# A time-mixing kernel: transposed input for batches 10 to 15 from the DMA crossbar, out of a staging copy in DRAM

## The chip, the cores and the metric

The kernel runs on one core of a Trainium2 chip. A core has five instruction streams that matter here: TensorE (PE: matmuls and, against an identity matrix, transposes), VectorE (DVE), ScalarE (ACT), GpSimd (POOL) and SyncE (SP, which only issues transfers). Sixteen DMA engines move data; SP's transfers go out on one queue, POOL's on another; in this kernel POOL's loads convert fp32 to bf16 on the way. The metric is device time in microseconds, the median of several runs.

## The reference

The input `x` has 16 batches of 2048 tokens with 256 features, in fp32. Cut to what matters:

```python
x_prev[:, 1:, :] = x[:, :-1, :]                 # the token before, zero for the first
xv = x * time_mix_v + x_prev * (1 - time_mix_v)
xr = x * time_mix_r + x_prev * (1 - time_mix_r)
v = xv @ value_weight
r = xr @ receptance_weight
out = (sigmoid(r) * v) @ output_weight
```

The key branch (`xk`, `k`) feeds nothing that is returned.

## The kernel before, in words

**Units.** A unit is 512 tokens, a quarter of a batch; there are 64, and the main loop runs over them with index `g`. Matmuls contract over the features, so `x` is needed with features on the partitions: each unit is transposed into a tile `xt`, in bf16. A batch of `xt` has a slot for each 128 tokens and one slot ahead of them, which holds the last 128 tokens moved on by one (the shift); with it, "the token before" is the same tile read one slot earlier.

**Per unit.** The weights carry the mix factors, so what is left to form is `mix = xt(previous) * c + xt`, for `r` and for `v`. One half of the products is scaled on DVE (line 271) or, late in the kernel, on ACT (line 530), the other half on POOL (line 281, `scale_pool`); DVE adds (line 293). Then PE projects (line 301), ACT takes the sigmoid (line 550), DVE multiplies (line 603), PE multiplies by the output weight (line 325), ACT copies the result to SBUF (line 359) and SP stores a pair of units (line 335).

**Two ways to transpose.** For units 1 to 43 PE transposes six units ahead of use (`advance`, `transposes`, line 215), and ACT copies from PSUM (line 232). For the last five batches (`BYDMA`, 20 units) the crossbar of the DMA engines transposes whole batches from the bf16 input tile in SBUF to `xt`: `by_dma`, line 196, issued by SP at units 38, 39, 43, 47 and 51. The first of them, batch 11, is split in two and waits for the last load of all. From unit 38 (`CROSS`) on, ACT does the shift of a batch (line 569) and some of the scales.

**Order.** The order of each engine's instructions is written by hand: an engine takes them in program order and waits at each for what it needs. So an instruction that waits on SP holds up the stores behind it, and one that waits on POOL holds up the scales behind it. `load(b)` is issued by POOL (lines 107 to 120); input tiles have six buffers, so batch `b+5` is loaded when batch `b` begins to be transposed. `WAITING` holds back some stores to set their order against the transposes; `kept` holds them till then. The pools: `xpool` 6 batches of input, `xtpool` 3 batches of `xt`, `opool` 3 batches of output.

Of the kernel before, what the change touches and what calls it, by code (L numbers as in the profile page):

```python
# [8 lines left out]
FP32 = mybir.dt.float32  # L9
BF16 = mybir.dt.bfloat16  # L10
# [5 lines left out]
def kernel(  # L16
# [25 lines left out]
    nc = tc.nc  # L42

    B, S, D = x.shape
    P = 128
    KO = D // P
# [6 lines left out]
    BYUNIT = 2  # L53
    LONG = 8
    H = UJ // 2
    BYDMA = 5 * UB
    CROSS = NU - BYDMA - LOOK
    FREE = CROSS
    LATE_O = CROSS - 2
    WAITING = {33: 38, 35: 39, 37: 43, 39: 43, 45: 51, 47: 51}  # L60
    START_T = [1, 3, 5, 6, 7, 9, 11, 12]
    AHEAD = 6
    PAIRS = 10
    WARM = 25
    WARM2 = 7
    SHIFT_ACT = (8,)

    consts = ctx.enter_context(tc.tile_pool(name="consts", bufs=1))
    xpool = ctx.enter_context(tc.tile_pool(name="xpool", bufs=6))
    xtpool = ctx.enter_context(tc.tile_pool(name="xtpool", bufs=3))  # L70
    mixpool = ctx.enter_context(tc.tile_pool(name="mixpool", bufs=3))
    zpool = ctx.enter_context(tc.tile_pool(name="zpool", bufs=3))
    opool = ctx.enter_context(tc.tile_pool(name="opool", bufs=3))
    ps_t_pool = ctx.enter_context(tc.tile_pool(name="ps_t", bufs=2, space=bass.MemoryType.PSUM))
    ps_v_pool = ctx.enter_context(tc.tile_pool(name="ps_v", bufs=1, space=bass.MemoryType.PSUM))
    ps_r_pool = ctx.enter_context(tc.tile_pool(name="ps_r", bufs=1, space=bass.MemoryType.PSUM))
# [6 lines left out]
    shifted = []  # L83
    kept = {}
    x_bf = {}
    xt = {}
    mix = {}
    o_sb = {}
# [9 lines left out]
    def rows(b):  # L98
        return x[b].rearrange("(p j) d -> p j d", p=P)

    def unit_rows(t, b, e, n=1):

        return t[b, e * TU : (e + n) * TU, :].rearrange("(e p j) d -> p e j d", p=P, j=UJ)

    def load(b):
        if b not in x_bf:
            x_bf[b] = xpool.tile([P, J, D], BF16, name="x_bf")
        if b < BYUNIT:
            for e in range(UB):
                nc.gpsimd.dma_start(  # L110
                    out=x_bf[b][:, e * UJ : (e + 1) * UJ, :], in_=unit_rows(x, b, e)[:, 0]
                )
            return
        if b < B - 1:
            run = 8192 if b < LONG else 16384
            return nc.gpsimd.dma_start(out=x_bf[b], in_=rows(b), max_dma_last_dim=run)  # L116
        return [
            nc.gpsimd.dma_start(out=x_bf[b][:, j : j + J // 2], in_=rows(b)[:, j : j + J // 2])
            for j in (0, J // 2)
        ]  # L120

    x_unit = opool.tile([P, 2, UJ, D], FP32, name="o_sb")
    tm_rows = consts.tile([2 * KO, P], FP32)
# [21 lines left out]
    w_bf = consts.tile([P, 2, KO, D], BF16)  # L145
    w_prev = consts.tile([P, KO, D], BF16)
    wo_bf = consts.tile([P, KO, D], BF16)
    x_first = consts.tile([P, 2, UJ, D], BF16)
    for e in (2, 3):
        op = nc.gpsimd.dma_start(out=x_first[:, e - 2], in_=unit_rows(x, 0, e)[:, 0])  # L150
        if e == 2:
# [11 lines left out]
    warm_up(WARM)  # L163

    def new_xt(b):
        if b < BYUNIT:
            xt[b] = consts.tile([P, UB * (UJ + 1), KO, P], BF16, name=f"xt_first{b}")
        else:
            xt[b] = xtpool.tile([P, J + 1, KO, P], BF16, name="xt")
        (nc.vector if b == 0 else nc.gpsimd).memset(xt[b][:, 0, :, 0:1], 0.0)  # L170

    new_xt(0)
# [18 lines left out]
        nc.vector.reciprocal(c_sb, tms)  # L191
        nc.vector.tensor_scalar(out=c_sb, in0=c_sb, scalar1=-1.0, scalar2=None, op0=ALU.add)

    def by_dma(b, lo, hi, after=None):

        op = nc.sync.dma_start_transpose(
            out=xt[b][:, 1 + lo : 1 + hi].rearrange("p j k c -> p (j k) c"),
            in_=x_bf[b][:, lo:hi].rearrange("p j d -> p (j d)"),
        )
        if after is not None:  # L200
            tc.add_manual_dep(op.ins, after.ins.name, SYNC, reason="not beside a load")

    def transposes(i):

# [125 lines left out]
                stop=(ko == KO - 1),  # L330
            )

    def store(queue, b, lo, hi, after=None):
        dst = out[b].rearrange("(p j) d -> p j d", p=P)
        op = queue.dma_start(out=dst[:, lo:hi, :], in_=o_sb[b][:, lo:hi, :])
        if after is not None:
            tc.add_manual_dep(op.ins, after.ins.name, SYNC, reason="in turn with the last load")

    def out_part(pool, name, z, b, e, jj, n, copy, queue):
        ps = pool.tile([P, n, D], FP32, name=name)  # L340
        for k in range(n):
            out_matmuls(ps, z, jj + k, k)
        lo = e * UJ + jj
        copy(out=o_sb[b][:, lo : lo + n, :], in_=ps)
        store(queue, b, lo, lo + n)

    def output(g, z):
        b, e = divmod(g, UB)
        if e == 0:
            o_sb[b] = opool.tile([P, J, D], FP32, name="o_sb")  # L350
        j0 = e * UJ
        if g >= NU - 4:
            for h in range(2):
                out_part(ps_t_pool, "ps_t", z, b, e, h * H, H, nc.scalar.copy, nc.sync)
            return
        ps = ps_o_pool.tile([P, UJ, D], FP32, name="psum_o")
        for jj in range(UJ):
            out_matmuls(ps, z, jj, jj)
        nc.scalar.copy(out=o_sb[b][:, j0 : j0 + UJ, :], in_=ps)  # L359
        if b < BYUNIT:  # L360
            if e % 2 == 1:
                nc.sync.dma_start(
                    out=unit_rows(out, b, e - 1, 2),
                    in_=o_sb[b][:, j0 - UJ : j0 + UJ, :].rearrange("p (e j) d -> p e j d", j=UJ),
                )
        elif g >= NU - 8:
            store(nc.sync, b, j0, j0 + UJ)
        elif e % 2 == 1:
            pair = (b, j0 - UJ, j0 + UJ)
            if g in WAITING:  # L370
                kept.setdefault(WAITING[g], []).append(pair)
            else:
                store(nc.sync, *pair)

    def last_unit(g):


        b, e = divmod(g, UB)
        s_sb = zpool.tile([P, KO, TU], BF16, name="s_sb")
        z_sb = zpool.tile([P, KO, TU], BF16, name="z_sb")  # L380
        cols = [(h * H * P, (h + 1) * H * P) for h in range(2)]
        spare = [(ps_r_pool, "psum_r"), (ps_t_pool, "ps_t"), (ps_v_pool, "psum_v"), (ps_t_pool, "ps_t")]
        banks = [pool.tile([P, KO, H * P], FP32, name=name) for pool, name in spare]

        by_act, by_dve = nc.scalar.copy, nc.vector.tensor_copy

        def receptance(h):
            lo, hi = cols[h]
            project(banks[h], g, 0, lo, hi)
            nc.scalar.activation(out=s_sb[:, :, lo:hi], in_=banks[h], func=ACT.Sigmoid)  # L390

        def value(h, n):
            lo, hi = cols[h]
            project(banks[2 + h], g, 1, lo, hi)
            for c in range(lo, hi, n * P):
                nc.vector.tensor_tensor(
                    out=z_sb[:, :, c : c + n * P],
                    in0=s_sb[:, :, c : c + n * P],
                    in1=banks[2 + h][:, :, c - lo : c - lo + n * P],
                    op=ALU.mult,  # L400
                )

        receptance(0)
        out_part(ps_o_pool, "psum_o", z_prev, b, e - 1, 0, H, by_dve, nc.sync)
        receptance(1)
        value(0, H)
        out_part(ps_r_pool, "psum_r", z_prev, b, e - 1, H, H, by_act, nc.sync)
        value(1, 1)
        out_part(ps_v_pool, "psum_v", z_sb, b, e, 0, 1, by_act, nc.sync)
        out_part(ps_o_pool, "psum_o", z_sb, b, e, 1, 1, by_act, nc.sync)  # L410
        out_part(ps_t_pool, "ps_t", z_sb, b, e, 2, 1, by_act, nc.scalar)
        out_part(ps_t_pool, "ps_t", z_sb, b, e, 3, 1, by_dve, nc.sync)
# [34 lines left out]
            tc.add_manual_dep(op.ins, after.ins.name, SYNC, reason="one at a time")  # L447

    tnext = 1
    half_load = last_load = None  # L450

    def advance(limit):
        nonlocal tnext, half_load, last_load
        while tnext <= min(limit, NU - 1):
            b, e = divmod(tnext, UB)
            if b == 1 and e > 0:
                load(b + e + 1)
            elif b > 1 and e == 0 and b + 5 < B:
                if b == 2:
                    load(6)  # L460
                last_load = load(b + 5)
                if b + 5 == B - 1:
                    half_load, last_load = last_load
            if tnext < NU - BYDMA:
                transposes(tnext)
            tnext += 1
# [71 lines left out]
    for g in range(NU - 1):  # L538
# [10 lines left out]
        s_sb = zpool.tile([P, KO, TU], BF16, name="s_sb")  # L549
        nc.scalar.activation(out=s_sb, in_=ps_r, func=ACT.Sigmoid)  # L550
        advance(START_T[g] if g < len(START_T) else g + LOOK)
        for b in range(B - 5, B):
            if g == max(UB * (b - 2) - 1, CROSS + (b > B - 5)):
                new_xt(b)
                if b == B - 5:
                    for pair in kept.pop(g):
                        store(nc.sync, *pair, after=half_load)
                    by_dma(b, J - UJ, J, last_load)
                    by_dma(b, 0, J - UJ, last_load)
                else:  # L560
                    by_dma(b, 0, J)
                for pair in kept.pop(g, []):
                    store(nc.sync, *pair)
        by_crossbar = g // UB + 1 if g > CROSS and g % UB == 1 and g < NU - UB else None

        def shift(ko):
# [83 lines left out]
```

## Time and profile before

| | |
|---|---|
| median of 3 runs | 201.58 us (201.2 to 202.09) |
| span of the profiled execution | 199.3 us; a time of the whole call is not listed for that execution |
| PE busy | 194.5 us, 98% |
| DVE busy | 186.1 us, 93% |
| ACT busy | 180.6 us, 91% |
| POOL busy | 83.7 us, 42% |
| SP's DMA queue (q1) | 40.24 MB, 59.0% of 16 engines' span |
| POOL's DMA queue (q0) | 16.39 MB, 41.1% |

The span runs from the first to the last instruction. Busy times are unions over an engine's instructions, so a share near 100% says that the engine hardly stood idle, not that each instruction was at its best. A DMA queue's share is the time that its packets took; the two together come to the whole span. Times to landing are from issue to the last byte's arrival and contain the wait in the queue: the median load of 1024 KB took 24.2 us, the median pair's store 14.4, the median transpose 7.6.

### The profile page before, as it was taken

The numbers are of one execution on the slowest core, as the hardware profiler recorded it, in microseconds if no ns is written. First come the engines' busy times: TensorE is split into PE (matmuls) and PEld (weight loads), VectorE is DVE, ScalarE is ACT, GpSimd is POOL, SyncE is SP. The second block draws the span as 40 slices with busy tenths as digits, with TensorE's granted clock in tenths as the row PEclk, the third lists the DMA queues.
The fourth block names the chain that finished last, engine by engine and source line by source line (L and its number), as shares of the span: only waits on it lengthen the run. The fifth ranks groups of instructions, "written<-read, shape, count | busy, mean of one in ns | idle before, by whom it ended". The sixth has DMA issues, their size and how long they took to land.

```text
span 199.3 us, 3892 instructions
## 1 busy us (share of the span) xinstructions
PE 194.5 (98%) x1421; PEld 125.8 (63%) x1421; DVE 186.1 (93%) x292; ACT 180.6 (91%) x209; POOL 83.7 (42%) x114
## 2 busy tenths in 40 slices
PE   8999999999999999999999999999999999999993
PEld 7765676666666666666666666555666566655671
DVE  0999999999999999899999999999999999999982
ACT  3699899999999999999999999999999999999982
POOL 1846572443443534425434354343444444444200
PEclk9999999999999999999999999999999999999998
DMA  5999999999999999999999999999999999999685
GB/s 182 228 194 217 218 277 275 278 280 274 292 313 293 283 283 288 280 284 284 281 286 337 299 409 294 300 199 226 287 294 396 301 210 261 419 418 409 266 313 213
DMA packets 32442, 57.00 MB, mean 286 GB/s; under 512 B 21796, under 2 KB 23080, under 8 KB 28456
## 3 DMA queue, kind: packets, MB, share of 16 engines
q1 hardware_dynamic: 28208, 40.24, 59.0%
q0 software_dynamic: 4064, 16.39, 41.1%
q8 instruction: 11, 0.18, 0.4%
q10 hardware_dynamic: 152, 0.13, 0.2%
q14 instruction: 7, 0.06, 0.1%
HBM read 34.34 MB, written 33.55 MB: 341 GB/s over the span
## 4 chain that ended last, share of the span: by engine, by line
PE 85%; DVE 10%; issue 1%; POOL 1%; ACT 1%; DVEq 0%; POOLq 0%
PE psum_v L301 25%; PE psum_o L325 24%; PE psum_r L301 24%; PE ps_t L215 7%; DVE z_sb L603 4%; DVE mix L293 3%; DVE mix L271 3%; PE ps_t L161 2%; PE ps_t L325 1%; PE psum_r L243 1%; ACT xt_first L225 1%; PE psum_r L315 0%; PE ps_t L301 0%; POOL x_bf L116 0%; POOL mix L281 0%
## 5 line engine op out<-in xcount | busy, mean ns | idle before, releaser
L281 POOL TENSOR_SCALAR mix<-xt,c_sb 128x1024 bf16<-128x1024 bf16 (+1 forms) x55 | 61.0, 1109 | 91.7 <-DVE mix L293 86.2
L293 DVE TENSOR_TENSOR mix<-mix,xt 128x1024 bf16<-128x1024 bf16 x112 | 77.8, 703 | 1.6
L603 DVE TENSOR_TENSOR z_sb<-s_sb,psum_v 128x1024 bf16<-128x1024 bf16 (+1 forms) x64 | 76.6, 1199 | 2.3 <-PE psum_v L301 0.9
L301 PEld LDWEIGHTS <-w_bf 128*128 128x128 bf16 x516 | 48.7, 98 | 38.9 <-DVE mix L293 1.1
L550 ACT ACTIVATE s_sb<-psum_r 128x1024 bf16<-128x1024 f32 x63 | 65.1, 1033 | 3.6 <-PE psum_r L301 3.3
L359 ACT COPY o_sb<-psum_o 128x1024 f32<-128x1024 f32 x60 | 61.2, 1021 | 6.0 <-PE psum_o L325 6.0
L301 PE MATMUL psum_v<-mix,w_bf 128*128 128x512 bf16 (+1 forms) x256 | 65.3, 377 | 0.5 <-DVE mix L293 0.2
L301 PE MATMUL psum_r<-mix,w_bf 128*128 128x512 bf16 (+1 forms) x252 | 64.2, 377 | 0.1
L325 PE MATMUL psum_o<-wo_bf,z_sb 128*128 128x256 bf16 x486 | 63.2, 272 | 0.0
L325 PEld LDWEIGHTS <-z_sb 128*128 128x128 bf16 x512 | 49.8, 98 | 19.7 <-issue 0.9
L232 ACT COPY xt<-ps_t 128x1024 bf16<-128x1024 bf16 x36 | 36.8, 1033 | 0.0
L215 PEld LDWEIGHTS <-x_bf 128*128 128x128 bf16 x320 | 21.0, 98 | 8.5
L215 PE MATMUL ps_t<-ident,x_bf 128*128 128x128 bf16 x320 | 23.9, 219 | 0.0
L271 DVE TENSOR_SCALAR mix<-xt,c_sb 128x1024 bf16<-128x1024 bf16 (+1 forms) x49 | 22.0, 458 | 0.0
L530 ACT ACTIVATE mix<-xt,c_sb 128x1024 bf16<-128x1024 bf16 x12 | 13.9, 1159 | 0.0
L293 DVE TENSOR_TENSOR mix<-mix,xt_first 128x1024 bf16<-128x1024 bf16 x15 | 10.8, 722 | 0.1
L116 POOL DMA_DIRECT2D x_bf<-in_x_dram x13 | 8.6, 659 | 0.0
L271 DVE TENSOR_SCALAR mix<-xt_first,c_sb 128x512 bf16<-128x512 bf16 x22 | 6.9, 364 | 0.4 <-ACT xt_first L225 0.3
L232 ACT COPY xt_first<-ps_t 128x1024 bf16<-128x1024 bf16 x6 | 6.2, 1028 | 0.0
L281 POOL TENSOR_SCALAR mix<-xt_first,c_sb 128x512 bf16<-128x512 bf16 x6 | 4.1, 684 | 1.6 <-DVE mix L293 1.0
L161 PE MATMUL ps_t<-const-bfloat16-1.0 128*128 128x128 bf16 x32 | 3.8, 312 | 0.8 <-PEq L634 0.8
L443 POOL COPY xt_first<-xt_first 128x254 bf16<-128x254 bf16 x5 | 2.0, 393 | 5.4 <-DVE mix L293 5.3
(70 smaller groups left out, 52.6 us busy)
## 6 DMA issues: line engine op xcount, KB each, us to landing
out_dram<-o_sb SPq DMA_DIRECT2D x28, 1024.0 KB, 14.4
x_bf<-in_x_dram POOLq DMA_DIRECT2D x13, 1024.0 KB, 24.2
out_dram<-o_sb SPq DMA_DIRECT2D x4, 512.0 KB, 2.9
out_dram<-o_sb SPq DMA_DIRECT2D x6, 256.0 KB, 2.5
o_sb<-in_x_dram SPq DMA_DIRECT2D x4, 256.0 KB, 3.6
x_bf<-in_x_dram POOLq DMA_DIRECT2D x4, 256.0 KB, 7.0
x_bf<-in_x_dram POOLq DMA_DIRECT2D x2, 512.0 KB, 10.7
x_first<-in_x_dram POOLq DMA_DIRECT2D x2, 256.0 KB, 4.3
```

Source lines behind the costliest of these rows:

```text
L116: return nc.gpsimd.dma_start(out=x_bf[b], in_=rows(b), max_dma_last_dim=run)
L215: nc.tensor.transpose(out=ps[:, jj], in_=src[:, jj, ko * P : (ko + 1) * P], identity=idn)
L232: nc.scalar.copy(out=xt[b][:, j0 : j0 + UJ], in_=ps)
L271: nc.vector.tensor_scalar(out=mixed(piece)[:, :, ko], in0=xt[b][:, slots(piece), ko], scalar1=c_sb[:, m, ko : ko + 1], scalar2=None, op0=A ...
L281: op = nc.gpsimd.tensor_scalar(out=mixed(piece)[:, :, 1], in0=xt[b][:, slots(piece), 1], scalar1=c_sb[:, m, 1:2], scalar2=1.0, op0=ALU.mul ...
L293: return nc.vector.tensor_tensor(out=mixed(piece), in0=mixed(piece), in1=xt[b][:, slots(piece, 1)], op=ALU.add)
L301: nc.tensor.matmul(out=ps[:, mo, :], lhsT=w_bf[:, m, ko, mo * P : (mo + 1) * P], rhs=mixed((b, m, e * TU + lo, e * TU + hi))[:, :, ko], st ...
L325: nc.tensor.matmul(out=ps[:, slot, :], lhsT=z[:, ko, jj * P : (jj + 1) * P], rhs=wo_bf[:, ko, :], start=(ko == 0), stop=(ko == KO - 1),)
L359: nc.scalar.copy(out=o_sb[b][:, j0 : j0 + UJ, :], in_=ps)
L530: nc.scalar.activation(out=mixed(piece)[:, :, ko], in_=xt[b][:, slots(piece), ko], func=ACT.Copy, scale=c_sb[:, m, ko : ko + 1],)
L550: nc.scalar.activation(out=s_sb, in_=ps_r, func=ACT.Sigmoid)
L603: nc.vector.tensor_tensor(out=z_sb[:, :, c : c + n], in0=s_sb[:, :, c : c + n], in1=ps_v[:, :, c : c + n], op=ALU.mult,)
```

## The change

Six batches instead of five, 10 to 15, go by the crossbar (24 units, so `CROSS` becomes 34). They are no longer loaded into SBUF: POOL's converting load writes them to a tile in DRAM, `x_both`, one for two batches. One transposing transfer takes the 256 rows of such a pair and writes a tile `xt_both` that interleaves the two batches in each slot (128 elements of one, 128 of the other). PE's transposes for the other batches from 2 on write tiles of that form too.

The pair transposes are issued by SP at units 31, 39 and 47 (`T_AT`); each waits for the load issued last. Batches 14 and 15 are loaded at units 35 and 43 (`STAGE_AT`); these loads, on POOL, wait for the transpose issued last. The other loads follow a table (`LOADS`). Output tiles hold two units instead of a batch (nine of them) and are allocated with that size; `xpool` has 4 buffers, one of which first serves as `x_first`; `xtpool` has 2 of double width.

```diff
-    BYDMA = 5 * UB
+    STAGED = 10
+    BYDMA = NU - STAGED * UB
-    WAITING = {33: 38, 35: 39, 37: 43, 39: 43, 45: 51, 47: 51}
+    T_AT = {31: 10, 39: 12, 47: 14}
+    WAITING = {27: 31, 29: 31, 33: 39, 35: 39, 41: 47, 43: 47}
+    STAGE_AT = {35: (14,), 43: (15,)}
+    LOADS = {
+        (1, 1): (3,), (1, 2): (4,), (2, 0): (5,), (3, 0): (6,), (4, 0): (7,),
+        (5, 0): (8, 10), (6, 0): (9,), (7, 0): (11, 12), (8, 0): (13,),
+    }
-    xpool = ctx.enter_context(tc.tile_pool(name="xpool", bufs=6))
-    xtpool = ctx.enter_context(tc.tile_pool(name="xtpool", bufs=3))
+    xpool = ctx.enter_context(tc.tile_pool(name="xpool", bufs=4))
+    dpool = ctx.enter_context(
+        tc.tile_pool(name="dpool", bufs=(B - STAGED) // 2, space=bass.MemoryType.DRAM)
+    )
+    xtpool = ctx.enter_context(tc.tile_pool(name="xtpool", bufs=2))
-    opool = ctx.enter_context(tc.tile_pool(name="opool", bufs=3))
+    opool = ctx.enter_context(tc.tile_pool(name="opool", bufs=9))
...
     def load(b):
-        if b not in x_bf:
+        if b >= STAGED:
+            if b % 2 == 0:
+                x_both[b] = dpool.tile([2, P, J, D], BF16, name="x_both")
+            x_bf[b] = x_both[b - b % 2][b % 2]
+        else:
             x_bf[b] = xpool.tile([P, J, D], BF16, name="x_bf")
...
     def new_xt(b):
+        if b >= BYUNIT:
+            if b % 2:
+                return
+            xt_both[b] = xtpool.tile([P, J + 1, KO, 2, P], BF16, name="xt_both")
+            for k in range(2):
+                xt[b + k] = xt_both[b][:, :, :, k]
+                nc.gpsimd.memset(xt[b + k][:, 0, :, 0:1], 0.0)
+            return
...
-    def by_dma(b, lo, hi, after=None):
+    def by_dma(b, after):
+        new_xt(b)
         op = nc.sync.dma_start_transpose(
-            out=xt[b][:, 1 + lo : 1 + hi].rearrange("p j k c -> p (j k) c"),
-            in_=x_bf[b][:, lo:hi].rearrange("p j d -> p (j d)"),
-        )
-        if after is not None:
-            tc.add_manual_dep(op.ins, after.ins.name, SYNC, reason="not beside a load")
+            out=xt_both[b][:, 1:].rearrange("p j k b c -> p (j k) (b c)"),
+            in_=x_both[b].rearrange("b p j d -> (b p) (j d)"),
+        )
+        tc.add_manual_dep(op.ins, after.ins.name, SYNC, reason="not beside a load")
+        return op
...
-        for b in range(B - 5, B):
-            if g == max(UB * (b - 2) - 1, CROSS + (b > B - 5)):
...
+        if g in T_AT:
+            last_t = by_dma(T_AT[g], last_load)
+        for pair in kept.pop(g, []):
+            store(nc.sync, *pair)
+        for b in STAGE_AT.get(g, ()):
+            last_load = load(b)
+            tc.add_manual_dep(last_load.ins, last_t.ins.name, SYNC, reason="not beside transposes")
```

## The prediction

> **What bounds the kernel now.** I read the busy tenths of the page first, then windows by stage, then the chain, then SP's and POOL's rows and the DMA issues.
>
> ```profile
> PE   8999999999999999999999999999999999999993
> DVE  0999999999999999899999999999999999999982
> PEclk9999999999999999999999999999999999999998
> DMA  5999999999999999999999999999999999999685
> HBM read 34.34 MB, written 33.55 MB: 341 GB/s over the span
> 80.00:100.00 20.00, 20.00 (x158) 13.22 (x157) 18.86 (x28) 18.58 (x20) 8.45 (x9) 1.00 1.03 284
> 140.00:150.00 10.00, 10.00 (x62) 5.89 (x61) 9.99 (x15) 9.54 (x13) 4.09 (x6) 1.00 1.07 292
> ```
>
> The window columns are PE, PEld, DVE, ACT and POOL busy, granted clock, DMA share, GB/s. PE never waits and its clock is full; in the late stage DVE is full too (9.99 of 10). The DMA engines are full in nearly every slice as well, so a transfer moved or added can't be called free.
>
> ```profile
> 97.09 0.45 PE ps_t L215 x8
> 98.40 0.87 PE psum_o L325 x8
> 101.44 0.87 PE psum_o L325 x8
> 104.49 0.55 PE psum_o L325 x5
> ...
> 142.37 0.87 PE psum_o L325 x8
> 144.97 0.87 PE psum_o L325 x8
> 147.57 0.91 PE psum_o L325 x8
> ```
>
> The chain gives the price of a unit. With TensorE transposing, output follows output after (104.49-98.40)/2 = 3.045 us; by the crossbar, 2.60 (142.37 to 147.57: two units in 5.20). The difference is the eight transposes, 0.45 us.
>
> ```profile
> 133.38 4.87 SPq L196 DMA_TRANSPOSE xt<-x_bf  x1
> 162.56 4.85 SPq L196 DMA_TRANSPOSE xt<-x_bf  x1
> GB/s 289 289 297 294 292 119 18 49 138 184 236 197 218 205 207 228 215 202 236 210 202 236 215 205 238 207 210 233 215 207 233 210 212 230 215 207 225 220 210 223
> x_bf<-in_x_dram POOLq DMA_DIRECT2D x1, 1024.0 KB, 17.3
> x_bf<-in_x_dram POOLq DMA_DIRECT2D x1, 1024.0 KB, 12.9
> 136.63 1.12 POOL L281 TENSOR_SCALAR mix<-xt,c_sb 128x1024 bf16<-128x1024 bf16 x1 [1.40 <-DVE mix L293]
> 141.80 1.12 POOL L281 TENSOR_SCALAR mix<-xt,c_sb 128x1024 bf16<-128x1024 bf16 x1 [1.25 <-PE psum_v L301]
> 144.55 1.12 POOL L281 TENSOR_SCALAR mix<-xt,c_sb 128x1024 bf16<-128x1024 bf16 x1 [1.63 <-DVE mix L293]
> 145.50 1.30 DVE L293 TENSOR_TENSOR mix<-mix,xt 128x1024 bf16<-128x1024 bf16 x2
> 177.47 0.30 ACT L569 COPY xt<-xt 128x127 bf16<-128x127 bf16 x1
> ```
>
> SP spends 4.85 us on a 1 MB transpose. The GB/s row (163 to 167 us, 0.1 us a slice) is crossbar traffic alone: about 216 in the steady stretch, which is SP's pace, 1.05 MB in 4.85 us, but 290 in a short burst at its head, while descriptors were waiting. The two loads are batches 13 and 14 (issued at 90.76 and 102.89, landed at 108.0 and 115.8). The rest gives deadlines, below.
>
> **The change, part by part.** *Off TensorE:* units 40 to 43 lose 32 transposes and four ACT evacuations of 1.03 us (L232), two DVE scales of 0.47 (ACT takes them, two of 1.16) and a 0.22 shift copy (ACT: two of 0.3). Per unit that is the stage switch the chain shows: 4 x (3.045-2.605) = **-1.76 us**. It is the most there is: PE's 2.60 are matmuls, and DVE is full at the same period.
>
> *Strided tiles.* A batch's slots now lie 256 elements apart, so the add (681 ns) and ACT's copy read or write runs of 128. The scale reads such runs already, at 474. I take nothing for the add; the upper end is its slowest usual row (773): 92 ns x 2 adds x 30 late units = 5.5 us on a full DVE; below nothing no row points.
>
> *Loads.* Batches 0 to 13 are issued by the same unit (26) as before, with four buffers for six and batches 10 to 13 going DRAM to DRAM. Before, the queue never ran dry up to batch 13; after it doesn't either: the shortest queue is when batch 8 is issued near 54.6, with batches 6 and 7 (issued at 32.6 and 42.5, before both near 25.5) barely through or still under way, since a load takes about 7.5 us of the queue. So batch 13 still lands near 108 if a staged load costs what a load costs. Batch 9 is needed at 102.9, four places earlier in the queue: no wait. Smaller output tiles, their earlier allocation and held stores add no instruction to a full engine; nine pairs of units against six leave more room for late stores.
>
> *The serial part.* Transpose (10,11), load 14, transpose (12,13), load 15, transpose (14,15) now wait for each other, through SP, which holds stores behind a waiting transpose (no engine needs them soon), and through **POOL**, whose scales stand behind the waiting load. Late stage times are those of before less 4 x 3.045 = 12.2 us.
> - Slack on POOL: an odd unit's scale can start 2.1 us late (the next starts after 1.63 idle and ends at 145.67, its reader is the second add of 145.50, at 146.15). At unit 35 it is due at 131.37-12.2 = 119.2, so with the load's own 0.6 us transpose (10,11) must land by 119.2+2.1-0.6 = **120.7**; at unit 43, transpose (12,13) by 152.24-12.2+1.5 = **141.5**; transpose (14,15) by ACT's shift, 177.47-12.2 = **165.3**.
> - Cost R of 2.1 MB through the crossbar: SP's pace gives 2 x 4.85 = 9.7; the 290 GB/s of the burst gives 7.2. Ends: 5.0 (stores reach 418 GB/s) and 11.2. The upper one is the transpose of 139.42 to 146.12, which first waited for POOL's memset at 140.44-140.55: 5.6 a batch. No row has a source in DRAM. I take **7.2**: source and destination both in SBUF is what sets SP's pace here, the engines are shown to do more when fed; 9.7 stays in the range.
> - First: issue 108.1 after load 13, one pair's store ahead (2.2 us), R, and 1.9 from SP's end to landing (133.38+4.87 to the landing 6.8 after issue): 112.2+R = 119.4. In time.
> - Second: load 14, 10 us (12.9 beside stores all along; 7.5 is its pace in a full queue; three stores are queued here), about 1 to start, R, 1.9: 125.1+2R = 139.5, in time.
> - Third: the same again with four stores, 11 us: 139+3R = 160.6, in time.
> R may be 8.2 before anything waits. Sum: -1.76, **197.5 us of span**. The profiled execution's span is 199.3; the median, 201.58, lies 2.3 above it, which I take to lie around the span unchanged: **199.8 us**, 0.9% less.
>
> A page says otherwise. The Trainium skill, "DMA: Bandwidth & Descriptors", "Why small descriptors are slow (HBM only)", charges small packets in HBM 11 cycles for 8 at 256 B, and spares SBUF to SBUF. The profile has 256 B packets for the transposes only from SBUF, so no run here shows it yet; by the rule the burst's rate would become 211 GB/s, R an estimated 9.9, and the change would cost about 1.6. Its section "Latency and other measured facts" has 261 GB/s for a transpose, an estimate of 8.0 for R, and the sum of -1.76 would stand.
>
> **Rivals.**
> 1. *SP's pace stays, R = 9.7.* For: two issues of equal length. Against: the burst. Landings 121.9, 144.5, 168.1: late by 1.2, then 1.8 more, nothing more at the third (168.3 by then). 3.0-1.76: 202.8. The lateness is 2R-16.4 from R = 8.5 on, so the change turns slower at R = 9.1.
> 2. *The crossbar reads DRAM worse than SBUF, R = 11.2.* Landings 123.4, 147.5 and 172.6: late by 2.7, 3.3 and 1.3: 7.3-1.76, 207.1.
> 3. *Staged loads are slower.* For: up to 100 us loads read 280 GB/s from DRAM beside 140 of stores, 420 in all, as much as stores alone reach; were that a limit on DRAM traffic of both directions, a staged load's 1.05 MB written too would make 7.5 into 10 us. Four of them put load 13 at 118. Transpose (10,11) then lands near 128 (7.5 late), the second near 150 (1.3 more): 8.8-1.76, 208.6. Against: 341 GB/s over the span proves no limit.
> 4. *Partly late:* R of 8.5 to 9.3 costs 0.6 to 2.2, loads of 12.9 at R = 7.2 cost 1.1: about 201.2.
> 5. *The strided add slows* by 20 to 90 ns: 201 to 205.
>
> **How the numbers follow.** No wait 0.47; rival 1 0.16, rival 2 0.08, rival 3 0.11, rival 4 0.13, rival 5 0.05. The bound for a change is 0.5%, 1.0 us: all of the first case is faster (0.46 with a little for its own spread); rival 4 and parts of 1 and 5 are within it (0.15); slower 0.39. If nothing waits, the range is 199.3 to 200.5. Over all cases low is 199.3, and high 206.5 leaves out rival 3, most of 2: under 0.2.
>
> **What would show it.** Right: the period of 2.6 us from unit 34, near 115.5, no DVE wait on POOL around 119 and 140, L220 taking 7 to 8 us, three landings near 119, 140 and 161. Wrong: POOL's load rows (L138) at units 35 and 43 held up, with DVE's add waiting for L305 behind them; L220 at 10 us or more; batch 13 landing after 110; the add above 700 ns.

## The result, and the profile after

The changed kernel takes **208.42 us** (median of 4 runs, 207.63 to 209.18) beside 201.39 for the kernel before on the same chip: ratio 1.0355, 95% interval 1.0316 to 1.0394. Predicted were 199.8 us and a range up to 206.5. Here and below, medians are over all executions, while ratios and intervals leave out those more than 1.5% above the fastest of the same kernel. The profiled span is 206.1 us, 6.8 more than the 199.3 before. In the lines below, of the changed kernel's profile, the new line numbers are: L138 a load, L220 the pair transpose, L305 POOL's scale, L317 DVE's add, L325 the projections, L349 the output matmul, L385 ACT's copy of the output, L584 ACT's shift, L618 DVE's product.

The page's busy tenths:

```profile
PE   8999999999999999999999999999499996999990
...
DVE  1899999999999999999999999999589998899970
...
PEclk9999999999999999999999999999969999999998
DMA  5899999999999999999999999879999999999994
...
HBM read 34.34 MB, written 39.85 MB: 360 GB/s over the span
...
L317 DVE TENSOR_TENSOR mix<-mix,xt_both 128x1024 bf16<-128x1024 bf16 x112 | 78.5, 712 | 3.5 <-POOL mix L305 2.1
```

Before, PE and DVE had no slice under 8 between the start and the end. Now there is a hole at 144 to 149 us (a slice is 5.15 us), with the granted clock down to 6 tenths in the slice behind it, and a second hole at 170 to 175. 6.3 MB more are written to HBM (39.85 against 33.55), the three staged pairs. The same windows as before, and three more (PE, PEld, DVE, ACT and POOL busy, granted clock, DMA share, GB/s):

```profile
80.00:100.00 20.00, 20.00 (x158) 13.23 (x157) 18.86 (x28) 18.58 (x21) 8.49 (x10) 1.00 1.02 284
140.00:150.00 10.00, 7.34 (x44) 4.09 (x43) 7.84 (x10) 6.71 (x10) 3.46 (x4) 0.99 1.15 362
150.00:160.00 10.00, 10.00 (x55) 5.73 (x53) 8.65 (x13) 8.13 (x9) 3.87 (x6) 0.84 0.99 265
170.00:180.00 10.00, 8.31 (x53) 5.00 (x52) 8.26 (x12) 7.84 (x10) 3.67 (x4) 1.00 1.08 400
180.00:190.00 10.00, 10.00 (x63) 5.88 (x61) 9.91 (x15) 9.54 (x13) 4.40 (x4) 1.00 1.01 417
```

80 to 100 us is unchanged. PE loses 2.66 us in one window and 1.69 in another; between them it is busy for all of 150 to 160, but at a clock of 0.84 and with fewer instructions (55, 63 in the undisturbed window). The chain of work that ended last (start, duration, what) says what PE stood waiting for:

```profile
114.70 0.92 PE psum_o L349 x8
115.61 0.86 PE psum_v L325 x4
116.48 0.86 PE psum_r L325 x4
117.34 0.87 PE psum_o L349 x8
...
132.11 1.01 ACT o_sb L385
133.18 0.81 DVE z_sb L618
133.99 10.64 DMA xt_both<-x_both
144.67 0.47 issue
145.16 0.56 POOL x_both L138
145.76 1.13 POOL mix L305
146.91 1.62 DVE mix L317
148.58 1.04 PE psum_r L325 x4
...
159.69 12.84 DMA xt_both<-x_both
172.75 1.01 ACT o_sb L385
```

The period of 2.6 us is there from unit 34 on (114.70 to 117.34), as predicted. But where the chain of before is PE from start to end here, now two transposes stand in it, of 10.64 and 12.84 us from issue to landing, and the first hands over to POOL's load, then POOL's scale, DVE's add and PE: exactly the path that the prediction drew for a late transpose. POOL's rows at the two loads (the bracket is its idle time before; it is put down to DVE, but what the load waits for is the transpose, which landed 0.5 us earlier):

```profile
121.11 0.55 POOL L138 DMA_DIRECT2D x_both<-in_x_dram  x1 [3.04 <-DVE mix L317]
145.16 0.56 POOL L138 DMA_DIRECT2D x_both<-in_x_dram  x1 [5.49 <-DVE z_sb L618]
```

Taking unit after unit by DVE's product, the time goes like this. Up to unit 34 the kernels keep step (116.8 us both). Then come stalls of 0.7 us at unit 36 (POOL's load 14), 4.5 at units 44 to 46 (load 15, with the slow clock behind it) and 1.9 at unit 53 (ACT's shift waiting for the last transpose), 7.1 in all. Against them stand the 1.76 us of the transposes of units 40 to 43, which were gained (they show at the products of units 34 to 37, since PE transposed six units ahead). The way from the last whole product (unit 62) to the end grew from 8.0 to 9.35 us. 7.1 - 1.76 + 1.3 = 6.6, and 0.2 to 0.4 from a later start.

The chain of transfers, issue to landing, in us:

| | issue | landing | took | predicted |
|---|---|---|---|---|
| load 13 | 90.95 | 107.86 | 16.9 | landing near 108 |
| transpose (10,11) | 108.06 | 120.58 | 12.5 | 11.3 |
| load 14 | 121.11 | 133.85 | 12.7 | 10 |
| transpose (12,13) | 133.99 | 144.63 | 10.6 | 10.1 |
| load 15 | 145.16 | 159.54 | 14.4 | 11 |
| transpose (14,15) | 159.69 | 172.53 | 12.8 | 10.1 |

### The profile page after: what moved, and what is told of

Same layout as the page of the kernel before. It is cut to its first block, busy times and chain, and to the rows that moved or that the text cites. A ratio compares the mean times of both kernels' runs of the same rounds, so it can differ in the third digit from the quotient of the medians.

```text
span 206.1 us, 3819 instructions
## 1 busy us (share of the span) xinstructions
PE 195.3 (95%) x1389; PEld 124.1 (60%) x1389; DVE 186.1 (90%) x289; ACT 179.7 (87%) x209; POOL 83.2 (40%) x113
## 2 busy tenths in 40 slices
DMA packets 36298, 58.05 MB, mean 282 GB/s; under 512 B 25780, under 2 KB 27064, under 8 KB 32184
## 3 DMA queue, kind: packets, MB, share of 16 engines
HBM read 34.34 MB, written 39.85 MB: 360 GB/s over the span
## 4 chain that ended last, share of the span: by engine, by line
PE 68%; DMA 14%; DVE 8%; issue 3%; ACT 3%; POOL 2%; SPq 0%; DVEq 0%; ACTq 0%; POOLq 0%
PE psum_v L325 20%; PE psum_r L325 19%; PE psum_o L349 19%; DMA xt_both<-x_both 11%; PE ps_t L239 8%; DVE z_sb L618 3%; DVE mix L317 3%; DMA w_f<-n_receptance_weight_dram 2%; ACT o_sb L385 2%; PE ps_t L349 1%; DVE mix L295 1%; PE psum_r L339 1%; POOL mix L305 1%; ACT mix L550 1%; PE ps_t L325 0%
## 5 line engine op out<-in xcount | busy, mean ns | idle before, releaser
L305 POOL TENSOR_SCALAR mix<-xt_both,c_sb 128x1024 bf16<-128x1024 bf16 (+1 forms) x55 | 61.3, 1115 | 87.7 <-DVE mix L317 82.7
L317 DVE TENSOR_TENSOR mix<-mix,xt_both 128x1024 bf16<-128x1024 bf16 x112 | 78.5, 712 | 3.5 <-POOL mix L305 2.1
L618 DVE TENSOR_TENSOR z_sb<-s_sb,psum_v 128x1024 bf16<-128x1024 bf16 (+1 forms) x64 | 76.6, 1199 | 4.7 <-PE psum_v L325 3.2
L325 PEld LDWEIGHTS <-w_bf 128*128 128x128 bf16 x516 | 49.1, 99 | 44.1 <-DVE mix L317 5.4
L325 PE MATMUL psum_r<-mix,w_bf 128*128 128x512 bf16 (+1 forms) x252 | 64.6, 379 | 3.2 <-DVE mix L317 3.1
L325 PE MATMUL psum_v<-mix,w_bf 128*128 128x512 bf16 (+1 forms) x256 | 66.2, 381 | 0.2
L385 ACT COPY o_sb<-psum_o 128x1024 f32<-128x1024 f32 x60 | 61.4, 1023 | 5.5 <-PE psum_o L349 5.5
L349 PE MATMUL psum_o<-wo_bf,z_sb 128*128 128x256 bf16 x486 | 63.8, 274 | 1.7 <-ACT o_sb L385 1.7
L349 PEld LDWEIGHTS <-z_sb 128*128 128x128 bf16 x512 | 50.0, 98 | 21.6 <-issue 2.6
L256 ACT COPY xt_both<-ps_t 128x1024 bf16<-128x1024 bf16 x32 | 32.9, 1039 | 0.0
L239 PEld LDWEIGHTS <-x_bf 128*128 128x128 bf16 x304 | 19.6, 98 | 8.7 <-DMA x_bf<-in_x_dram 1.4
L239 PE MATMUL ps_t<-ident,x_bf 128*128 128x128 bf16 x304 | 22.7, 219 | 0.0
L295 DVE TENSOR_SCALAR mix<-xt_both,c_sb 128x1024 bf16<-128x1024 bf16 (+1 forms) x47 | 21.1, 458 | 0.8 <-ACT xt_both L584 0.8
L550 ACT ACTIVATE mix<-xt_both,c_sb 128x1024 bf16<-128x1024 bf16 x14 | 16.2, 1158 | 0.0
L317 DVE TENSOR_TENSOR mix<-mix,xt_first 128x1024 bf16<-128x1024 bf16 x15 | 10.6, 715 | 0.1
L138 POOL DMA_DIRECT2D x_both<-in_x_dram x6 | 3.4, 560 | 8.5 <-DVE z_sb L618 5.5
L138 POOL DMA_DIRECT2D x_bf<-in_x_dram x8 | 5.7, 712 | 0.0
L584 ACT COPY xt_both<-xt_both 128x127 bf16<-128x127 bf16 x12 | 3.7, 312 | 1.7 <-DMA xt_both<-x_both 1.7
```

Of the source, the lines that this page charges most:

```text
L239: nc.tensor.transpose(out=ps[:, jj], in_=src[:, jj, ko * P : (ko + 1) * P], identity=idn)
L256: nc.scalar.copy(out=xt[b][:, j0 : j0 + UJ], in_=ps)
L295: nc.vector.tensor_scalar(out=mixed(piece)[:, :, ko], in0=xt[b][:, slots(piece), ko], scalar1=c_sb[:, m, ko : ko + 1], scalar2=None, op0=A ...
L305: op = nc.gpsimd.tensor_scalar(out=mixed(piece)[:, :, 1], in0=xt[b][:, slots(piece), 1], scalar1=c_sb[:, m, 1:2], scalar2=1.0, op0=ALU.mul ...
L317: return nc.vector.tensor_tensor(out=mixed(piece), in0=mixed(piece), in1=xt[b][:, slots(piece, 1)], op=ALU.add)
L325: nc.tensor.matmul(out=ps[:, mo, :], lhsT=w_bf[:, m, ko, mo * P : (mo + 1) * P], rhs=mixed((b, m, e * TU + lo, e * TU + hi))[:, :, ko], st ...
```

## The experiments

My theory after the result: the serial chain costs the time, through waits that the change adds, and each of its steps is long because the stores that its waits let go get ahead of it. The rivals: POOL is the wrong place for the load; the crossbar reading DRAM is slow in itself; a load needs long to begin; or the DMA engines simply have no time left, so that a wait removed at one place comes back at another.

**Free both added waits.** The transposes no longer wait for the load issued last, nor the loads for the transpose; what data they need still orders them.

```diff
-        tc.add_manual_dep(op.ins, after.ins.name, SYNC, reason="not beside a load")
...
-            tc.add_manual_dep(last_load.ins, last_t.ins.name, SYNC, reason="not beside transposes")
```

> Both added waits are taken away (the transposes' wait for the load issued last, the staged loads' wait for the transpose issued last); the true waits stay. Theory A, the serial chain of five transfers sets the loss: transposes land near 118 to 122, 140 and 162, within the deadlines 120.7, 141.5 and 165.3, and the time is 199.8 to 200.8 us, below the kernel before. Rival B, POOL's queue is the cause: the same here, so this run does not part A from B. Rival C, the DMA engines are simply too full with staging added: transfers slow each other, landings stay late, 205 us or more.

201.5 us, ratio 1.0020 (1.0001 to 1.0039), span 199.7. Load 14 is issued at 117.49, while the first transpose is still under way, and load 15 at 138.30; POOL is not held. The three transposes land at 119.7, 145.1 and 166.0. One stall of 1.0 us is left, at unit 45 (ACT's shift, and PE behind it):

```profile
145.09 0.30 ACT L582 COPY xt_both<-xt_both 128x127 bf16<-128x127 bf16 x1 [0.88 <-DMA xt_both<-x_both]
...
146.35 1.03 PE L348 MATMUL psum_o<-wo_bf,z_sb 128*128 128x256 bf16 x8 [0.86 <-ACT o_sb L384]
```

So the two waits cost some 7 us. But the kernel comes out level with before, above the 199.8 to 200.8 expected: 1.0 in this stall, 1.35 in the tail (from unit 62's product to the end, 9.4 us). The second transpose was issued by SP behind three stores; in the window of 127 to 133 us the DMA queues show 2.41 MB on SP's queue at 98.1% of the engines' time, nearly all of it these stores, and its own packets begin only at 132.65. That is one part of its lateness. The other is load 15, which now runs beside it: the last data of the transpose ran at 141.7, but it landed only at 145.1, and from 142 to 145 us the queues show

```profile
q0 software_dynamic: 80, 0.66, 104.1%
q1 hardware_dynamic: 32, 0.00, 1.5%
```

The engines are full of the load, and of SP's queue only 32 packets of 4 B run. In the changed kernel, where no load ran beside them, the three transposes landed 0.5 us after their last data. With 0.5 here too it would have landed at 142.2, ahead of the shift, which could have begun at 144.2.

**Free one of the two.** Once only the load's wait is removed, once only the transpose's.

```diff
-            tc.add_manual_dep(last_load.ins, last_t.ins.name, SYNC, reason="not beside transposes")
```

> Only the staged loads' wait for the transpose is taken away, so POOL never waits there; each transpose still waits for the load issued last. A: load 14 is issued near 118 beside the first transpose and lands near 130, the second transpose lands near 141, load 15 is issued near 139 and lands near 151, the last transpose lands near 163: 200 to 201.5 us. C: 205 or more, with the first transpose landing after 125. B: 200 to 202, since POOL is free.

202.91 us, over ten executions that lie between 200.81 and 212.88, so the same program can take 12 us more or less; ratio 1.0051 (1.0018 to 1.0084), span 201.9; transposes land at 121.0, 146.3 and 168.3, with stalls at units 45 and 53.

```diff
-        tc.add_manual_dep(op.ins, after.ins.name, SYNC, reason="not beside a load")
```

> Only the transposes' wait for the load issued last is taken away; the staged loads still wait for the transpose on POOL. Theory A: the first transpose lands near 120, load 14 is issued near 120.7, the second transpose is issued at 127 and runs behind three stores and beside load 14, landing near 145; POOL waits for it from 139, which costs 2 to 4 us; load 15 lands near 156, the last transpose near 168: 204 to 206 us, between e1 and the changed kernel. If the transposes' wait is the main one, 201 to 202.

204.65 us, ratio 1.0208 (1.0142 to 1.0273), span 201.9; landings at 119.7, 141.8 and 168.3. POOL is still held at both loads:

```profile
120.21 0.61 POOL L138 DMA_DIRECT2D x_both<-in_x_dram  x1 [2.84 <-DVE z_sb L617]
142.37 0.57 POOL L138 DMA_DIRECT2D x_both<-in_x_dram  x1 [3.40 <-DVE mix L294]
```

Of the 3.55% that the change costs, 3.0 come back without the load's wait and 1.5 without the transpose's: the load's is the dearer, but either alone leaves a part. (The two profiled executions are equally long; that of the first kernel is among its longer ones.)

**The loads later in POOL's order**, at units 37 and 46, so that POOL reaches them after the transposes have landed.

```diff
-    STAGE_AT = {35: (14,), 43: (15,)}
+    STAGE_AT = {37: (14,), 46: (15,)}
```

> The two waits stay, but the staged loads stand later on POOL, at units 37 and 46 in place of 35 and 43, by when the transposes have landed, so that POOL has nothing to wait for. A, the chain: load 14 is issued near 124 in place of 121.1, so everything behind it comes 3 us later and more, and ACT and PE wait for the landings in place of POOL: 210 to 214 us. B, POOL's wait is the cause: 5 to 7 us are won back, 201 to 203.

209.46 us, ratio 1.0416 (1.0395 to 1.0437), no better than the change itself. POOL no longer holds up its scales, and the whole wait appears at the last transpose, which lands at 171.7:

```profile
171.73 0.30 ACT L584 COPY xt_both<-xt_both 128x127 bf16<-128x127 bf16 x1 [5.26 <-DMA xt_both<-x_both]
```

That POOL is the wrong place is out. POOL's block is only where the chain's lateness shows first.

**No loads in the chain.** Batches 14 and 15 are not loaded, and so their output is not computed.

```diff
-    STAGE_AT = {35: (14,), 43: (15,)}
+    STAGE_AT = {}
...
-            in_=x_both[b].rearrange("b p j d -> (b p) (j d)"),
+            in_=x_both[min(b, 12)].rearrange("b p j d -> (b p) (j d)"),
```

> Batches 14 and 15 are not loaded at all, and the last transpose reads the staged batches 12 and 13 again, so the output of the last two batches is left out. A: no transpose waits for a load after 108, the landings come near 120.6, 139.5 and 160: 199.5 to 200.5 us, the whole 1.76 us of four units. C, crossbar and strided tiles themselves cost it: over 202.

201.03 us, ratio 0.9985 (0.9953 to 1.0016), span 198.6. The transposes land at 119.1, 138.9 and 159.7, close to what was predicted (119.4, 139.5, 160.6), and there is no stall. The product of unit 62 comes 2.0 us earlier than before (189.27 against 191.27), of which 0.24 stand there from the first units on: the gain of the change is real, all 1.76 of it. The way from there to the end is 9.4 us, as in the run with both waits free, and takes 1.35 back, so the time misses the 199.5 to 200.5 expected. In SP's rows the transposes take:

```profile
107.21 9.83 SPq L220 DMA_TRANSPOSE xt_both<-x_both  x1
126.99 9.83 SPq L220 DMA_TRANSPOSE xt_both<-x_both  x1
147.84 9.84 SPq L220 DMA_TRANSPOSE xt_both<-x_both  x1
```

That is 4.9 us a batch, the pace of before (4.85) from SBUF: a source in DRAM is not slower, and the pace that I had taken to belong to SBUF tiles is there too.

**Stores moved**, first one of them, on top of the kernel with both waits free: the store of units 30/31 goes behind the second transpose.

```diff
-    WAITING = {27: 31, 29: 31, 33: 39, 35: 39, 41: 47, 43: 47}
+    WAITING = {27: 31, 29: 31, 31: 39, 33: 39, 35: 39, 41: 47, 43: 47}
```

> As e1, and the store of units 30 and 31 is issued by SP behind the second transpose (unit 39) in place of ahead of it. In e1 the second transpose was issued at 126.9 us, but its packets ran only from 132.7, behind three stores on the same queue; it landed at 145.1 and ACT's shift and PE waited 1.0 us for it. If stores ahead on the queue are the cause (theory Q), its packets start near 130 and land near 142.5, the wait goes and the time falls by 0.7 to 1.2 us against e1's 201.5: 200.3 to 200.8. If the sum of transfers is (theory C), the wait only moves, to the last transpose: 201.5 or more.

207.4 us, ratio 1.0269 (1.0206 to 1.0331), span 206.1. The second transpose's packets begin at 131.4 in place of 132.65. But its last data runs at 142.8 and it lands at 146.3, again with load 15 on the engines between the two, so ACT's shift still waits for it (1.13 us). The third's packets begin only at 160; it lands at 170.7, and ACT's shift waits there too:

```profile
170.72 0.30 ACT L582 COPY xt_both<-xt_both 128x127 bf16<-128x127 bf16 x1 [3.40 <-DMA xt_both<-x_both]
```

One store moved costs 2.5%, 5 us: the first wait stayed, and a second, longer one came to it. Theory C had the second, and neither that the first would stay.

**The chain kept, and the stores taken out from ahead of load 14.** Both added waits stay; three stores go behind the second transpose.

```diff
-    WAITING = {27: 31, 29: 31, 33: 39, 35: 39, 41: 47, 43: 47}
+    WAITING = {27: 39, 29: 39, 31: 39, 33: 39, 35: 39, 41: 47, 43: 47}
```

> Both added waits stay. Only the stores of units 26/27, 28/29 and 30/31 are moved: from between the first transpose and the second to behind the second, so that load 14 has no store ahead of it. Theory S (load 14 took 12.7 us because three stores, 3.1 MB, were let go just ahead of it; by itself a load begins within 2 us, as one did where it was issued during a transpose, and takes 5 to 6.6): load 14 lands 7 to 9 us after its issue, near 129, transpose (12,13) lands near 138 to 140, the stall of 4.5 us at units 44 to 46 is gone. Seven stores and load 15 then stand between the second transpose and the third, 18 us of stores at 2.6 each: load 15 takes 14 us or more, transpose (14,15) lands at 172 to 176 as before or later, and the stall there grows from 1.9 to 4 to 7. Span 202.5 to 206. Rival (a load waiting on POOL needs its 5.8 us to the first packet by itself): load 14 again 12 to 13 us, transpose (12,13) near 144 to 145, the stall at 44 to 46 again 4 to 5, the third later than 173 in addition: span 207 to 211.

Load 14 lands 7.6 us after its issue, at 128.6, and the second transpose at 140.4: as the theory on the loads had it (7 to 9 us, near 129, 138 to 140). The DMA queues of 121 to 127 us, first of the changed kernel, then of this one (queue, packets, MB, share of the engines' time; q1 is SP's, q0 POOL's):

```profile
DMA packets 293, 2.14 MB, mean 356 GB/s; under 512 B 32, under 2 KB 32, under 8 KB 32
...
q1 hardware_dynamic: 291, 2.12, 100.2%
q0 software_dynamic: 2, 0.02, 1.3%
...
x_both<-in_x_dram POOLq DMA_DIRECT2D x1, 1024.0 KB, 12.7
```

```profile
DMA packets 109, 0.89 MB, mean 149 GB/s; under 512 B 0, under 2 KB 0, under 8 KB 0
...
q0 software_dynamic: 109, 0.89, 81.0%
...
x_both<-in_x_dram POOLq DMA_DIRECT2D x1, 1024.0 KB, 7.6
```

In the changed kernel, stores hold all 16 engines for the first 5.8 us after the load's issue, and the load has two packets through; without them it is almost done in that time. Yet the kernel takes 212.44 us, ratio 1.0571 (1.0516 to 1.0626), span 210.4, worse than the change and outside the 202.5 to 206 I gave. The span fits the rival's 207 to 211, but its reason, a load that needs 5.8 us by itself, is refuted by the 7.6. The stores now stand ahead of load 15 (14.7 us) and the third transpose (18.5 us, landing at 174.25), and PE stands still:

```profile
175.54 1.86 PE L349 MATMUL psum_o<-wo_bf,z_sb 128*128 128x256 bf16 x8 [7.43 <-ACT o_sb L385]
177.20 1.91 PE L325 MATMUL psum_v<-mix,w_bf 128*128 128x512 bf16 x4
178.90 1.91 PE L325 MATMUL psum_r<-mix,w_bf 128*128 128x512 bf16 x4
180.61 1.20 PE L349 MATMUL psum_o<-wo_bf,z_sb 128*128 128x256 bf16 x8
```

My span was wrong because I let the last stall grow from the 1.9 us it has in the changed kernel. There, the earlier stalls have already moved the deadline; without them a landing at 174.25 is 9 us late, not 3.

**One store to the end**, both waits free: one store leaves the place ahead of the second transpose, one goes behind the third.

```diff
-    WAITING = {27: 31, 29: 31, 33: 39, 35: 39, 41: 47, 43: 47}
+    WAITING = {27: 39, 29: 31, 33: 39, 35: 47, 41: 47, 43: 47}
```

> Both added waits are off, as in the run that freed both (span 199.7: a stall of 1.0 us at unit 45 behind three stores queued ahead of transpose (12,13)). One of these three stores (units 26/27) goes behind transpose (12,13), and one from there (34/35) behind transpose (14,15), so that the second transpose has two stores ahead of it in place of three, the third as many as before, and the end one more. If the order of the stores alone costs what is left: packets of transpose (12,13) begin near 130 and it lands near 142, the stall of 1.0 goes, transpose (14,15) stays near 166, span 198.7 to 199.5, ratio 0.993 to 1.000. If the DMA engines have no time left anywhere from 108 us on, the store comes back as a wait elsewhere: at the last transpose (landing 168 or later, a stall of 1 to 3 near unit 53) or in the tail (10 us or more after the last product): span 199.7 to 202.5, ratio 1.000 to 1.012.

205.04 us, ratio 1.0166 (1.0118 to 1.0214), span 203.5, worse than either case I gave had its bounds. The stall at unit 45 is gone, as foreseen. In its place are 0.8 us at unit 37 (the first transpose's last data ran at 120.2, but it landed at 124.2, with load 14 on the engines between the two), 1.9 at unit 53 (landing 167.85), and a tail of 11.4 us. That fits DMA engines without room: here a store put off was paid for later.

**The tail.** 64 instructions fewer run on PE now (32 transposes, each with a weight load). PE's code comes over DMA in packets of 16 KB: 11 of them both before (2842 recorded PE instructions) and after (2778), so some 250 instructions each. The last one falls at 188.3 us before, 11 us from the end, but 6.7 us from the end in the changed kernel and in the run with both waits free. It holds one DMA engine for 0.9 to 1.1 us among the last stores. Stores left over from earlier are not needed for a long tail: in the run without the loads the engines stand idle from 186.6 to 187.6, and its tail is 9.4 us all the same. Two runs gave PE 48 instructions more, at its start, where it waits for data: 49 warm-up matmuls of 32x64 in place of 25 of 128x128. Once with both waits free, and once with the store of units 30/31 moved too.

```diff
-    WARM = 25
+    WARM = 49
...
-            nc.tensor.matmul(out=ps, lhsT=ones, rhs=ones, start=True, stop=True)
+            nc.tensor.matmul(out=ps[:w, :c], lhsT=ones[:, :w], rhs=ones[:, :c], start=True, stop=True)
```

> As e1, with 49 narrower warm-up matmuls in place of 25, which end at the same time: 48 more instructions on PE ahead of the first data. In e1 and e4 the last 16 KB fetch of PE's code came 6.8 us ahead of the end and blocked one DMA engine for 1.1 us among the last stores, which landed 3.1 us after issue; in the kernel before it came 11 us ahead of the end and the last stores took 2.0. If that is why the tail is longer (theory F), the fetch moves to some 10.7 us ahead of the end, the last store lands about 2.0 us after issue, and the time falls by 0.8 to 1.2 against e1: 200.3 to 200.8. If not, 201.5 as e1, with the last store at 3.1.

201.92 us, ratio 0.9999 (0.9961 to 1.0037), span 200.9 in the profiled execution, one of the longer ones. The last packet of code is 9.3 us from the end, the tail 8.8 us.

> Both edits of e5 and e6 on e1. Theories Q and F together: 199.3 to 199.8 us, some 0.7% below the kernel before, which is the 1.76 us of four units without the waits. If either fails, 200.3 to 200.8; if both, 201.5.

201.28 us, ratio 0.9986 (0.9957 to 1.0015), span 199.7: the best of the versions that compute everything, not told apart from before, and above the 199.3 to 199.8 expected. The last packet of code is 9.3 us from the end, the tail 8.6 us. The median times to landing of the three small stores at the end, in the window from 185 us, stand in order for the kernel before, the changed one and this one:

```profile
out_dram<-o_sb SPq DMA_DIRECT2D x3, 128.0 KB, 2.0
```

```profile
out_dram<-o_sb SPq DMA_DIRECT2D x3, 128.0 KB, 3.2
```

```profile
out_dram<-o_sb SPq DMA_DIRECT2D x3, 128.0 KB, 2.4
```

Half of the longer tail comes back with the earlier code packet (9.35 to 8.6, of 8.0 before). That supports the code packet as a cause, but no run moved it alone: in these two executions the start came later too. In the first run a piece of the first input landed later (PE went on with it at 5.82 us, at 4.87 before), in the second the first 512-wide matmuls were twice as long (1.06 us for two, 0.68 and 0.59 before), and the trace's first entry of PE's clock, at full, begins only at 9.49 us there, against 6.69 before, which fits a clock still low at the start. Two executions with the old warm-ups start 1.0 to 1.3 us late as well (load's wait free, and 30/31 behind), so this need not come from the new ones. The second run has the order of stores of the run which took 207.4, and comes only 0.5 us later than that one up to unit 45; yet its second transpose came in time and its third nearly (ACT waited 0.31 us). There the second transpose's last data ran at 138.7, ahead of load 15's issue at 139.8. Why these two kernels lie 6 us apart stays open.

**All runs on one line.** The last deadline was predicted at 165.3 us. Its lateness gives the span nearly by itself, counted from the run without the loads (198.6). Four executions (load's wait free, 30/31 behind, and the two with more warm-ups) run 0.7 to 1.2 us late from their start on, which is in both columns.

| run | ratio | transpose (14,15) lands | less 165.3 | span less 198.6 |
|---|---|---|---|---|
| the change | 1.0355 | 172.5 | 7.2 | 7.5 |
| both waits free | 1.0020 | 166.0 | 0.7 | 1.1 |
| load's wait free | 1.0051 | 168.3 | 3.0 | 3.3 |
| transpose's wait free | 1.0208 | 168.3 | 3.0 | 3.3 |
| loads later | 1.0416 | 171.7 | 6.4 | 8.9 |
| no loads | 0.9985 | 159.7 | early | 0 |
| 30/31 behind | 1.0269 | 170.7 | 5.4 | 7.5 |
| three stores behind | 1.0571 | 174.3 | 9.0 | 11.8 |
| one store to the end | 1.0166 | 167.9 | 2.6 | 4.9 |
| more warm-ups | 0.9999 | 167.8 | 2.5 | 2.3 |
| the same, 30/31 behind | 0.9986 | 166.9 | 1.6 | 1.1 |

Where the last wait is 3.4 us or more (loads later, 30/31 behind, three stores behind), 2 to 3 us come on top, most of them because PE's clock drops: four matmuls of a projection then take 1.91 us in place of 1.03. In the run with one store to the end, the 2 us on top are its tail.

## Why the prediction was wrong

*What was right.* The gain: 2.6 us a unit from unit 34 on, and all of -1.76 us in the run without loads. The strided add: 712 ns against 703, nothing on the path. The loads up to batch 13: 107.86 against "near 108", so staging in DRAM cost them nothing, and rival 3 falls. The path of a late transpose: through POOL's load, POOL's scale, DVE's add and PE. The deadlines: the last one, 165.3, gives the table above.

*The step that failed: "The serial part", its three landings.* Predicted were 119.4, 139.5 and 160.6, measured 120.6, 144.6 and 172.5. The lateness of the last, 11.9 us, is by its terms: load 14 "10 us" measured 12.7 (+2.7); load 15 "11 us" measured 14.4 (+3.4); the transposes, 11.3, 10.1 and 10.1, measured 12.5, 10.6 and 12.8 (+1.2, +0.5, +2.7); and the hand-overs, which I had put at nothing, 0.53 us each from a landing to POOL's issue and 0.15 to SP's (+1.35). With 4.7 us of slack at the last deadline, 7.2 are left. SP's rows at the first transpose:

```profile
108.06 10.52 SPq L220 DMA_TRANSPOSE xt_both<-x_both  x1
118.68 2.09 SPq L361 DMA_DIRECT2D out_dram<-o_sb  x3
```

- *The loads* carry half of it. I did see the stores queued beside them, and took 10 us from between 7.5 (a full queue) and 12.9. What I missed is the order that the wait itself makes: SP stands at the transpose with the stores behind it. It is through with the transpose 2.0 us before the landing (108.06 + 10.52 = 118.58) and goes on to the stores; POOL issues the load 0.5 us after the landing. Load 14 begins behind 3 MB of stores. Taking those away made it 7.6 us: shown for load 14. For load 15 there is only the same picture: from 145 to 151 us stores hold 100.2% of the engines' time, and the load has two packets through.
- *The transposes.* "I take 7.2", because SBUF on both sides was to set SP's pace, is refuted by the 9.83 us from DRAM. At times it does run faster: the crossbar reaches the 290 GB/s I had read from the burst, as below, and SP's share was 8.53 for the second transpose. What decides between the paces stays open, but the record shows where the time goes: in the head of a transpose, not in stores beside it. Of the third, only 0.2 MB had run by 165.0, 5.3 us after its issue, while from 161.2 to 165.0 the queues show no packets but its own (688 of 256 B, 0.18 MB); from 165.0 to 172.0 it moves some 290 GB/s, the pace I had forecast for the whole.
- *The chances.* I gave 0.16 to SP's pace, 0.13 to lateness in part, loads of 12.9 us among it, and 0.47 to nothing of the kind, as if they were separate matters. In a chain of five steps each is added to all behind it: 1.5 us more a step are 7 at the end. (Loads of 12.9 at R = 7.2 are late by 0.9 by the prediction's own terms, not 1.1.) Rivals 2 and 3 had the size of the time (207.1 and 208.6), but not its cause: DRAM as a source is not slower, and load 13 landed at 107.86, not 118. That their times come near is luck.

*The step "what lies around the span unchanged", and the tail in the span.* The part outside the span held (1.9 us in the changed kernel's profiled execution; I had 2.3). That the end itself grows by 1.3 us was in no part of the sum. With it, the forecast without any wait would have been 0.2% faster, and not to be told from no change. The run without the loads is just that: 0.9985.

*So even with the waits off, why not faster?* Of 1.76 us, the tail takes 1.3, and the rest goes into waits for late transposes. I read this as DMA engines that are the tighter resource from 108 us on; it is argued, not shown. The change gives TensorE time back, has the DMA engines move 1.05 MB more (58.05 MB against 57.00), and moves the last two loads, landed at 115.8 and 127.6 before, into the stretch from 121 to 160, between and beside the pair transposes. In three runs a store shifted out of the way of one transfer met another; in the fourth, with more warm-ups, it did not. And the added waits were not without use: without them a transpose can end beside a load, and then land 2.3 to 4.0 us after its last data. I found no version that beats the kernel before.

The GB/s of the changed kernel's second transpose, 133 to 145 us in 40 slices of 0.3 us:

```profile
GB/s 55 0 0 0 0 0 0 34 84 239 291 259 163 219 194 172 140 122 282 206 124 289 288 288 294 291 288 288 294 291 288 288 294 291 288 288 494 440 437 437
```

It has the engines to itself up to 143.5 us, and moves 288 to 294 from 139.3 us on, but 120 to 290 before that. The Trainium skill, "DMA: Bandwidth & Descriptors", section "Latency and other measured facts", has 261 GB/s for a transpose with a non-contiguous middle dimension, and 350 to 400 for a contiguous one; the steady part here lies between, and the mean over its packets' time (2.1 MB in 8.9 us, 236) below both. The rule in "Why small descriptors are slow (HBM only)", by which I had worked out an estimate of 211, is not what holds it: the same 256 B packets, read from DRAM, reach 290.

## What to carry to other kernels

A chain of transfers that wait for each other is priced with what its waits let go: a store held up behind a waiting transfer goes out the moment the wait ends, ahead of the next link. Add the lateness of all links up to the last deadline and take that as the cost; a stall seen earlier is only a part of it, paid in advance, so mending an early link moves the wait instead of removing it. And where DMA engines are full from end to end, count a change that gives an engine time and costs traffic as level at best until the place for the traffic is found, and count the last microseconds after the last product as a stage of its own.

## What the runs showed of the hardware

- After a wait of 2.66 us PE's granted clock fell to half, 1.2 us behind the wait (at 149.74), and stayed there for 3.41 us: in the changed kernel four matmuls of a projection took 1.91 us (at 150.87; 1.03 is usual), and the windows below show the clock. In the 7.43 us wait quoted above it fell before the wait ended, at 170.69, for 10.24 us, so PE worked at half clock for over 5 us at once. After the waits of 3.38 and 5.25 us (30/31 behind, loads later) it was half for 3.41 and 6.83 us: one, two or three times the same 3.41. A wait of 0.86 us left it alone. The Trainium skill, "TensorE: Matmul & The Clock Gate", Part 1, has half the clock after at least one idle window of about 3.4 us; here 2.66 us of idling were enough.

```profile
148.00:150.00 2.00, 1.42 (x8) 0.85 (x9) 2.00 (x3) 0.35 (x1) 0.69 (x1) 0.94 1.13 373
150.00:152.00 2.00, 2.00 (x9) 1.06 (x7) 1.97 (x4) 1.56 (x2) 0.43 (x1) 0.50 0.98 233
152.00:154.00 2.00, 2.00 (x9) 0.90 (x8) 1.11 (x1) 1.24 (x3) 1.20 (x3) 0.71 1.08 291
154.00:156.00 2.00, 2.00 (x15) 1.22 (x13) 1.58 (x4) 1.86 (x2) 0.52 (x1) 1.00 1.04 221
```

- A transpose can land late when a load ends beside it: 2.3 to 4.0 us after its last data in five cases (the second one with both waits free, with the load's wait free, with 30/31 behind and with more warm-ups; the first one with one store to the end), each with the load's packets on the engines between. In the other 28 pair transposes of these runs it was 0.5 to 0.6 us, some of them beside a load too.
- Removing PE instructions moved the arrival of its code: one packet of 16 KB for some 250 instructions, 0.9 to 1.1 us on one DMA engine. That this is felt where small stores are waited for is supported, not shown.
